# Attention on one core: where the second to fourth pairs' queries and keys are turned into fp16

## The chip, the cores and the metric

The kernel runs on one core of a Trainium2 chip. TensorE (PE) multiplies matrices and transposes, ScalarE (ACT) takes exponentials, VectorE (DVE) and GpSimd (POOL) do elementwise work, and SyncE (SP) issues transfers. The 16 DMA engines of the core move data between HBM and SBUF; transfers can be issued from SyncE, ScalarE or GpSimd, and one that changes the data type while it moves is issued from GpSimd here. The metric is the device time of one execution in microseconds.

## The reference

Attention over 8 batches of 8 heads, each with 512 queries and keys of 64 elements, in fp32:

```python
q, k, v: (8, 8, 512, 64) float32
scores = einsum('bhqd,bhkd->bhqk', q, k) / sqrt(64)
attn = exp(scores - scores.max(-1)); attn /= attn.sum(-1)
out = einsum('bhqk,bhkd->bhqd', attn, v)
```

## The kernel before

Two heads make a pair, g = 0 to 31. In each head the 512 keys are four chunks of 128. A unit is one chunk of one head: its scores, 128 keys by 512 queries, are one matmul on TensorE (`scores`, line 185). ScalarE takes the exponential of three units in one instruction (`softmax`, line 233); these groups are numbered j, and the first three are smaller. The result pt multiplies v (`weigh`, line 244, 16 products for a head), with a column of ones beside v that gives the sums; DVE divides (`normalise`, lines 257 and 258) and SyncE stores (`save`, line 266). Eight units are set aside from ScalarE and computed by polynomial on DVE with one step on GpSimd (`Aside`, lines 207 to 220); its result e is written at line 210.

For the scores, q and k must lie with the 64 elements across partitions. So the fp16 tile qk of a pair, 128 positions by 2 x 2 x 4 x 64, is transposed on TensorE (`transpose`, line 141: 16 small matmuls, those of q first, then those of k) into PSUM, and DVE copies it to tqk (line 144).

How qk and v come in:

- Pair 0: heads loaded in fp32 by SyncE and ScalarE (`load_head`), cast by several engines (`open_cast`, line 159).
- Pair 1: `load(1, "qk")` on SyncE (line 85), 256 KB each, and `cast_qk(1)` on GpSimd (line 113).
- Pairs from 2: `load_cast(g)` (line 93), two transfers issued from GpSimd that read fp32 and write fp16.
- v of every pair: `load(g, "v")` on SyncE, and `cast_v(g)` on GpSimd (line 121) into one of five buffers vps, from which the products of the pair five before must have been read.

Each engine works in the order in which the program gives it its instructions. Lines 399 to 449 write out the opening by hand. Then the loop over j (line 451) gives ScalarE its exponential, TensorE the scores of the next group, and at a pair's first unit a block: `load_cast(g + 6)`, `cast_v(g + 2)`, `load(g + 5, "v")`. `plan.fill(j)` then picks transposes, heads (products and division) and set-aside units from a table of estimated costs and times. Estimates decide the order when the program is built, and neither the transfers' queue nor their landing enters them; for the transposes a fixed time for each pair is used. In the order that comes out, the transposes of pair 2 stand on TensorE ahead of the scores of group 5, which belong to pair 1; those of pair 3 ahead of the scores of group 8; those of pair 4 behind the scores of group 9.

Of the kernel before, what the change touches and what calls it, by code (L numbers as in the profile page):

```python
# [27 lines left out]
def kernel(  # L28
# [34 lines left out]
    G = 3  # L63
    NV = 5
    AHEAD = 6

    cpool = ctx.enter_context(tc.tile_pool(name="att_const", bufs=1))
    lpool = ctx.enter_context(tc.tile_pool(name="att_load", bufs=AHEAD + 1))
    xpool = ctx.enter_context(tc.tile_pool(name="att_x", bufs=4))
# [4 lines left out]
    def rows(x, g, lo=0, hi=2):  # L74
        b, h = g // ppb, 2 * (g % ppb)
        return x[b, h + lo : h + hi].rearrange("h (p i) d -> p h (i d)", i=NI)
# [3 lines left out]
    def load(g, names="qkv"):  # L80
        if g >= n_pairs:
            return
        for nm in names:
            r = lpool.tile([P, 2, NI * D], FP32, tag=f"{nm}32", name=f"{nm}32_{g}")
            nc.sync.dma_start(out=r, in_=rows(dict(q=q, k=k, v=v)[nm], g))
            raw[g, nm] = r

    def load_cast(g):
        if g >= n_pairs:
            return  # L90
        qk = xpool.tile([P, 2, 2, NI, D], FP16, tag="qk", name=f"qk_{g}", bufs=AHEAD + 4)
        for n in range(2):
            nc.gpsimd.dma_start(  # L93
                out=qk[:, n].rearrange("p h i d -> p h (i d)"), in_=rows((q, k)[n], g)
            )
        halves[g] = qk

    def load_head(h, nm, eng):
        if ("head", h) not in raw:
            raw["head", h] = cpool.tile([P, 2 * NI, D], FP32, name=f"raw_0_{h}")  # L100
        lo = NI * "kq".index(nm)
        eng.dma_start(  # L102
            out=raw["head", h][:, lo : lo + NI].rearrange("p (o i) d -> p o (i d)", o=1),
            in_=rows(dict(q=q, k=k)[nm], 0, h, h + 1),
        )
# [4 lines left out]
    def cast_qk(g):  # L110
        qk = xpool.tile([P, 2, 2, NI, D], FP16, tag="qk", name=f"qk_{g}", bufs=AHEAD + 4)
        for n in range(2):
            nc.gpsimd.tensor_copy(
                out=qk[:, n].rearrange("p h i d -> p h (i d)"), in_=raw[g, "qk"[n]]
            )
        halves[g] = qk

    def cast_v(g):
        if g >= n_pairs:
            return  # L120
        nc.gpsimd.tensor_copy(  # L121
            out=vps[g % NV][:, :, :, 0:D],
            in_=raw[g, "v"].rearrange("p h (i d) -> p h i d", d=D),
        )

    def aux(shape, dt, name):
        return pspool.tile(shape, dt, tag="ps_x", bufs=2, name=name)
# [21 lines left out]
    def open_cast(h, eng, lo, hi):  # L149


        if ("x", h) not in raw:
            raw["x", h] = cpool.tile([P, N, D], FP16, name=f"x_0_{h}")
            f = cpool.tile([D, NI + 1, P], FP16, name=f"t_0_{h}")
            r = cpool.tile([D, FIRST, P], FP16, name=f"r_0_{h}")
            raw["t", h] = f, r
            keys = [r[:, c] for c in range(FIRST)] + [f[:, 0]]
            tqk[0, h] = (f[:, 1:].rearrange("d n p -> d (n p)"), keys)
        eng(out=raw["x", h][:, lo:hi], in_=raw["head", h][:, lo:hi])  # L159

    def open_turn(h, lo, hi, ps):
        for i in range(lo, hi):
            nc.tensor.transpose(ps[:, i - lo, :], raw["x", h][:, i, :], ident16)

    def open_copy(h, eng, lo, hi, ps):
        f, r = raw["t", h]
        t = f[:, lo - FIRST : hi - FIRST] if lo >= FIRST else r[:, lo:hi]
        eng(out=t, in_=ps[:, 0 : hi - lo])
# [7 lines left out]
    def scores(j):  # L176
        if j >= len(sizes):
            return
        if j not in st:
            st[j] = pspool.tile([P, G, S], FP32, tag="ps_st", bufs=2, name=f"st_{j}")  # L180
        for x in range(sizes[j]):
            g, c, h = units[firsts[j] + x]
            tq, tk = tqk[g, h]
            key = tk[c] if g == 0 else tk[:, c * P : (c + 1) * P]
            nc.tensor.matmul(st[j][:, x, :], key, tq, start=True, stop=True)  # L185
# [44 lines left out]
    def softmax(j):  # L230
        n = sizes[j]
        pt[j] = ppool.tile([P, G, S], FP16, tag="pt", name=f"pt_{j}")
        nc.scalar.activation(out=pt[j][:, 0:n], in_=st[j][:, 0:n], func=EXP, scale=scale)  # L233
# [46 lines left out]
    def close():  # L280
        o = pspool.tile([P, NI, W], FP32, tag="ps_st", bufs=2, name="o_last")
        weigh(last, 1, o, range(NI - 1))
        softmax(len(sizes) - 1)
        weigh(last, 1, o, [NI - 1])
        normalise(last, 1, o)
        save(last, 1, 1)
# [111 lines left out]
    with tc.manual_schedule():  # L398
        load_head(0, "q", nc.sync)
        load_head(0, "k", nc.scalar)  # L400
        load_head(1, "q", nc.sync)
        load_head(1, "k", nc.scalar)
        blank = cpool.tile([P, P], FP16, name="blank")
        nc.vector.memset(blank, 0.0)
        small = cpool.tile([P, 1], FP32, name="small")
        nc.vector.memset(small, 0.0)  # L406
        nc.scalar.activation(out=small, in_=small, func=EXP, scale=scale)
        ident16 = cpool.tile([P, P], FP16, name="ident16")
        make_identity(nc, ident16)
        load(1, "qk")  # L410
        for g in range(AHEAD - 1):
            load(g, "v")
        for n in range(NV):
            nc.vector.memset(vps[n][:, :, :, D:W], 1.0)
        def busy(tile, n):
            for _ in range(n):
                nc.tensor.matmul(tile[:, G - 1, 0:P], blank, blank, start=True, stop=True)  # L417

        busy(pspool.tile([P, G, S], FP32, tag="ps_st", bufs=2, name="warm"), 24)
        A, V, Y = nc.scalar.copy, nc.vector.tensor_copy, nc.gpsimd.tensor_copy  # L420
        open_cast(0, V, 3, 6)
        open_cast(0, A, 6, 8)
        open_cast(0, A, 0, 3)
        open_cast(1, Y, 0, 3)
        a1, a2 = (aux([D, N, P], FP16, f"open_{n}") for n in range(2))
        a3 = pspool.tile([D, N, P], FP16, tag="ps_st", bufs=2, name="open_2")
        open_turn(0, 3, 6, a1)
        open_turn(0, 6, 8, a2)
        open_turn(0, 0, 3, a3)
        open_copy(0, V, 3, 6, a1)  # L430
        open_copy(0, A, 6, 8, a2)
        open_cast(1, V, 3, 8)
        open_copy(0, V, 0, 3, a3)
        st[0] = pspool.tile([P, G, S], FP32, tag="ps_st", bufs=2, name="st_0")
        busy(st[0], 4)
        scores(0)
        scores(1)
        b1, b2 = (aux([D, N, P], FP16, f"open_{n + 3}") for n in range(2))
        open_turn(1, 3, 8, b1)
        open_turn(1, 0, 3, b2)  # L440
        open_copy(1, V, 3, 8, b1)
        open_copy(1, V, 0, 3, b2)
        load_cast(2)
        cast_qk(1)
        load_cast(3)
        cast_v(0)
        load_cast(4)
        cast_v(1)
        load_cast(5)

        for j in range(len(sizes) - 1):
            assert not plan.heads or plan.heads[0][2] > j - 7, (j, plan.heads[0])
            softmax(j)
            plan.exp(j)
            if j > 0:
                scores(j + 1)
                plan.scored(j + 1)
                if j == 2:
                    for n in range(2):
                        transpose(1, (n,))  # L460
                        plan.turned(1)
                for u in range(firsts[j - 1], firsts[j - 1] + sizes[j - 1]):
                    g, c, h = units[u]
                    if u == first_of[g]:
                        load_cast(g + AHEAD)
                        cast_v(g + 2)
                        load(g + AHEAD - 1, "v")
                    if c == (FIRST - 1 if g == 0 else NI - 1):
                        plan.heads.append((g, h, j - 1))
                plan.fill(j)  # L470
        plan.fill(len(sizes), last_call=True)
        close()
# [30 lines left out]
```

The softmax here doesn't subtract the row's maximum and nothing guards it: scores larger than these inputs give would overflow.

## Time and profile before

| what | value |
|---|---|
| median of 13 runs | 127.92 us (126.83 to 129.32) |
| the profiled execution | 127.47 us, span 125.7 us |
| ScalarE busy | 114.3 us, 91% of the span |
| TensorE busy | 110.7 us, 88% |
| VectorE busy | 85.6 us, 68% |
| GpSimd busy | 70.9 us, 56% |
| granted TensorE clock, mean | 0.966 |
| GpSimd's queue | 16320 packets, 7.87 MB |
| SyncE's queue | 18256 packets, 17.57 MB |

The span runs from the first to the last instruction; the execution's own time is 1.8 us longer. Engine times are sums of busy time and can overlap. In the rows shown below, the first number is the start in microseconds from the span's beginning, the second the duration; "out<-in" names tiles as the program does; "x8" means eight instructions in one row; square brackets give the idle time of the engine just before and what ended it. A row of transfers ends with the size of one and the median time from issue to landing.

### The profile page before, as it was taken

The page shows a single profiled execution, that of the slowest core. Times are in us where ns is not written, and L with a number is a line of the kernel's source. Part 1 is how long each engine was busy: PE and PEld are TensorE (multiplying, and loading weights), DVE is VectorE, ACT ScalarE, POOL GpSimd, SP SyncE. Part 2 cuts the span into 40 slices and gives each one's busy share as a digit, 9 for nine tenths or more (in the row PEclk, how much of TensorE's full clock was granted, in tenths as well). Part 3 has the DMA queues.
Part 4 walks back from the last instruction along what each step waited for, and adds up shares of the span by engine and source line. Part 5 has one row for each costly group of instructions (what it writes and reads, how often), then busy time and mean ns, then how long its engine had stood idle before and what let it go on. Part 6 is the DMA issues. An engine that isn't in the chain of part 4 may idle for free.

```text
span 125.7 us, 4402 instructions
## 1 busy us (share of the span) xinstructions
PE 110.7 (88%) x1820; PEld 66.8 (53%) x1820; DVE 85.6 (68%) x213; ACT 114.3 (91%) x90; POOL 70.9 (56%) x109
## 2 busy tenths in 40 slices
PE   6981999999889999998998999899998998999690
PEld 6620556555546556555555645466554554666270
DVE  0440257996986898597879769955898699465251
ACT  4593489999999999999999999999999999999980
POOL 2699990894991099179529908995099162100000
PEclk9997569999999999999999999999999999999997
DMA  4999999899999999999999998999999974224204
GB/s 124 287 331 275 205 193 203 238 144 262 204 198 170 312 247 164 250 285 145 231 250 232 208 239 264 199 261 248 276 275 156 230 199 166 89 83 167 89 13 154
DMA packets 34883, 25.97 MB, mean 207 GB/s; under 512 B 2096, under 2 KB 34864, under 8 KB 34864
## 3 DMA queue, kind: packets, MB, share of 16 engines
q0 software_dynamic: 16320, 7.87, 50.6%
q1 hardware_dynamic: 18256, 17.57, 44.1%
q8 instruction: 14, 0.23, 0.8%
q10 hardware_dynamic: 288, 0.26, 0.6%
q14 instruction: 5, 0.04, 0.1%
HBM read 25.17 MB, written 8.39 MB: 267 GB/s over the span
## 4 chain that ended last, share of the span: by engine, by line
ACT 62%; issue 16%; PE 9%; DMA 8%; DVE 1%; POOL 1%; ACTq 0%
ACT pt L233 62%; DMA qk<-in_k_dram 6%; PE o L244 4%; PE st L185 4%; DMA raw<-in_k_dram 2%; PE tps L141 1%; DVE osb L258 1%; POOL qk L93 1%; ACTq L102 0%; DVE rcp L257 0%; POOL x L159 0%; ACTq L233 0%
## 5 line engine op out<-in xcount | busy, mean ns | idle before, releaser
L233 ACT ACTIVATE pt<-st 128x1536 f16<-128x1536 f32 (+2 forms) x85 | 111.9, 1540 | 5.1 <-PE st L185 5.1
L185 PE MATMUL st<-tqk 64*128 64x512 f16 x240 | 49.4, 389 | 5.8 <-ACT pt L233 5.0
L244 PEld LDWEIGHTS <-pt 128*128 128x128 f16 x992 | 34.2, 99 | 19.3 <-issue 10.5
L244 PE MATMUL o<-vp,pt 128*128 128x65 f16 x976 | 39.4, 196 | 1.1 <-DVE osb L258 0.5
L144 DVE COPY tqk<-tps 128x1024 f16<-128x1024 f16 (+1 forms) x32 | 21.2, 670 | 11.6 <-PE tps L141 11.2
L258 DVE TENSOR_TENSOR osb<-o,rcp 128x256 f32<-128x256 f32 x63 | 26.8, 425 | 2.2
L121 POOL CAST vp<-v 128x512 f16<-128x512 f32 x32 | 21.8, 684 | 5.0 <-PE o L244 4.9
L257 DVE RECIPROCAL rcp<-o 128x4 f32<-128x4 f32 x63 | 11.3, 179 | 18.6 <-PE o L244 18.1
L141 PEld LDWEIGHTS <-qk 128*64 128x64 f16 x496 | 15.6, 112 | 15.4 <-issue 9.1
L141 PE MATMUL tps<-ident,qk 128*64 128x128 f16 x496 | 20.4, 226 | 3.7 <-DMA qk<-in_q_dram 2.0
L93 POOL DMA_DIRECT2D qk<-in_q_dram x30 | 22.1, 735 | 0.4
L210 POOL TENSOR_SCALAR e<-n 128x512 int32<-128x512 int8 x8 | 4.9, 611 | 29.9 <-DVE n L207 29.9
L93 POOL DMA_DIRECT2D qk<-in_k_dram x30 | 21.6, 719 | 0.0
L185 PEld LDWEIGHTS <-tqk 64*128 64x128 f16 x240 | 11.5, 94 | 14.1 <-issue 6.5
L220 DVE SCALAR_TENSOR_TENSOR a<-f 128x512 f32<-128x512 f32 x8 | 6.9, 856 | 0.0
L220 DVE SCALAR_TENSOR_TENSOR pa<-a,f 128x512 f16<-128x512 f32 x8 | 6.1, 768 | 0.0
L220 DVE SCALAR_TENSOR_TENSOR f<-sa,n 128x512 f32<-128x512 f32 x8 | 5.5, 691 | 0.3
L220 DVE SCALAR_TENSOR_TENSOR f<-f,e 128x512 f32<-128x512 f32 x8 | 5.5, 681 | 0.0
L207 DVE TENSOR_SCALAR n<-sa 128x512 int8<-128x512 f32 x8 | 5.4, 681 | 0.0
L417 PE MATMUL warm<-blank 128*128 128x128 f16 x24 | 2.7, 313 | 1.0 <-DVE small L406 1.0
L417 PEld LDWEIGHTS <-blank 128*128 128x128 f16 x28 | 2.7, 141 | 1.1 <-DVE small L406 1.0
L244 PEld LDWEIGHTS <-pa 128*128 128x128 f16 x32 | 1.4, 98 | 3.4 <-DVE tqk L144 1.3
(32 smaller groups left out, 21.5 us busy)
## 6 DMA issues: line engine op xcount, KB each, us to landing
v<-in_v_dram SPq DMA_DIRECT2D x32, 256.0 KB, 5.7
out_dram<-osb SPq DMA_DIRECT2D x31, 256.0 KB, 4.4
qk<-in_q_dram POOLq DMA_DIRECT2D x30, 128.0 KB, 5.6
qk<-in_k_dram POOLq DMA_DIRECT2D x30, 128.0 KB, 6.1
raw<-in_k_dram ACTq DMA_DIRECT2D x2, 128.0 KB, 2.9
raw<-in_q_dram SPq DMA_DIRECT2D x2, 128.0 KB, 2.7
q<-in_q_dram SPq DMA_DIRECT2D x1, 256.0 KB, 4.7
k<-in_k_dram SPq DMA_DIRECT2D x1, 256.0 KB, 4.9
```

Of the source, the lines that this page charges most:

```text
L93: nc.gpsimd.dma_start(out=qk[:, n].rearrange("p h i d -> p h (i d)"), in_=rows((q, k)[n], g))
L121: nc.gpsimd.tensor_copy(out=vps[g % NV][:, :, :, 0:D], in_=raw[g, "v"].rearrange("p h (i d) -> p h i d", d=D),)
L141: nc.tensor.transpose(ps[D * h : D * (h + 1), n - lo, i, :], halves[g][:, n, h, i, :], ident16)
L144: nc.vector.tensor_copy(out=turned[g][:, lo:hi], in_=ps)
L185: nc.tensor.matmul(st[j][:, x, :], key, tq, start=True, stop=True)
L207: nc.vector.tensor_scalar(out=n, in0=s, scalar1=rate, scalar2=SHIFT, op0=AluOp.mult, op1=AluOp.add)
L220: nc.vector.scalar_tensor_tensor(out=o, in0=x, scalar=k, in1=y, op0=op0, op1=op1)
L233: nc.scalar.activation(out=pt[j][:, 0:n], in_=st[j][:, 0:n], func=EXP, scale=scale)
L244: nc.tensor.matmul(o[:, i, :], p[:, i * P : (i + 1) * P], vps[g % NV][:, h, c, :], start=(c == 0 and i == blocks[0]), stop=(c == NI - 1), ...
L257: nc.vector.reciprocal(out=rcp[:, lo:hi], in_=o[:, lo:hi, D:W])
L258: nc.vector.tensor_tensor(out=o_sb[g][:, h, lo:hi], in0=o[:, lo:hi, 0:D], in1=rcp[:, lo:hi].broadcast_to([P, hi - lo, D]), op=AluOp.mult,)
L417: nc.tensor.matmul(tile[:, G - 1, 0:P], blank, blank, start=True, stop=True)
```

## The change

A constant `WIDE = 4` divides the pairs. Queries and keys of pairs 2 and 3 (the third and fourth) no longer come by `load_cast` on GpSimd's queue; as for pair 1, SyncE loads them in fp32 and GpSimd casts them with `cast_qk`. The loads of q, k and v are interleaved on SyncE: q and k of 1, v of 0, q and k of 2, v of 1, q and k of 3, v of 2, 3, 4. Casting loads start with pair 4. In the opening GpSimd now gets: casts of pair 1, v of 0, casts of pair 2, v of 1, casting loads of 4 and 5. The casts of pair 3 stand at the head of pair 0's block, and in every block the cast of v now stands before the casting load.

```diff
     AHEAD = 6
+    WIDE = 4
...
         load(1, "qk")
-        for g in range(AHEAD - 1):
+        load(0, "v")
+        for g in range(2, WIDE):
+            load(g, "qk")
+            load(g - 1, "v")
+        for g in range(WIDE - 1, AHEAD - 1):
             load(g, "v")
...
-        load_cast(2)
         cast_qk(1)
-        load_cast(3)
         cast_v(0)
-        load_cast(4)
+        cast_qk(2)
         cast_v(1)
-        load_cast(5)
+        for g in range(WIDE, AHEAD):
+            load_cast(g)
...
                     if u == first_of[g]:
+                        if g + 3 < WIDE:
+                            cast_qk(g + 3)
+                        cast_v(g + 2)
                         load_cast(g + AHEAD)
-                        cast_v(g + 2)
                         load(g + AHEAD - 1, "v")
```

## The prediction

> **What bounds the kernel now.** I read the page first, then ScalarE's and TensorE's timelines of the first 25 us, then GpSimd's, and last the DMA issues one by one. ScalarE is 91% busy (114.3 of 125.7 us). Its timeline shows where the other time is:
>
> ```profile
> 6.78 3.79 ACT L233 ACTIVATE pt<-st 128x1024 f16<-128x1024 f32 x3 [0.29 <-PE st L185]
> 14.28 2.79 ACT L233 ACTIVATE pt<-st 128x1536 f16<-128x1536 f32 x2 [3.71 <-PE st L185]
> 17.55 2.92 ACT L233 ACTIVATE pt<-st 128x1536 f16<-128x1536 f32 x2 [0.47 <-PE st L185]
> 20.64 25.63 ACT L233 ACTIVATE pt<-st 128x1536 f16<-128x1536 f32 x19 [0.17 <-PE st L185]
> ```
>
> Columns: start, duration, what, and in brackets the idle time before it and its releaser. From 20.64 on the exponentials follow each other without a gap until 118.8. So what is lost before 20.64 is lost for good, and what is saved there is saved in the end: 3.71 + 0.47 + 0.17 = 4.35 us is the most that can be had. Exponential 5 (three units of pair 1; I number them by the loop variable j) starts at 14.28 and waits for scores that TensorE writes late. TensorE's timeline says why:
>
> ```profile
> 11.09 0.50 PE L141 MATMUL tps<-ident,qk 128*64 128x128 f16 x8 [2.01 <-DMA qk<-in_q_dram]
> 12.65 0.64 PE L141 MATMUL tps<-ident,qk 128*64 128x128 f16 x8 [1.06 <-DMA qk<-in_k_dram]
> 13.21 1.46 PE L185 MATMUL st<-tqk 64*128 64x512 f16 x6
> 14.61 1.94 PE L244 MATMUL o<-vp,pt 128*128 128x65 f16 x32
> 16.48 1.03 PE L185 MATMUL st<-tqk 64*128 64x512 f16 x3
> 17.44 0.94 PE L141 MATMUL tps<-ident,qk 128*64 128x128 f16 x16
> 18.31 0.60 PE L185 MATMUL st<-tqk 64*128 64x512 f16 x3
> ```
>
> The scores of exponential 5 belong to pair 1, which is long there, but in TensorE's order they stand behind the transposes of g=2 (third pair), and those wait for q and k of g=2. The chain that ended last goes the same way, and GpSimd's timeline has the issues:
>
> ```profile
> 5.45 7.15 DMA qk<-in_k_dram
> ...
> 12.65 0.64 PE tps L141 x5
> ```
>
> ```profile
> 4.57 0.88 POOL L93 DMA_DIRECT2D qk<-in_q_dram  x1
> 5.45 0.72 POOL L93 DMA_DIRECT2D qk<-in_k_dram  x1
> 6.36 0.61 POOL L113 CAST qk<-q 128x512 f16<-128x512 f32 x1 [0.19 <-DMA q<-in_q_dram]
> 7.05 0.62 POOL L113 CAST qk<-k 128x512 f16<-128x512 f32 x1
> ...
> 9.04 0.63 POOL L121 CAST vp<-v 128x512 f16<-128x512 f32 x1
> ```
>
> The casting loads are issued late (behind a cast that waits for the head of k) and take 6.5 and 7.15 us to land, at 11.04 and 12.60. A second loss hangs on the first: the granted clock is halved in the stretch after the wait.
>
> ```profile
> 4.45:11.28 6.83, 4.59 (x48) 2.19 (x48) 2.25 (x7) 5.24 (x6) 6.55 (x11) 1.00 1.13 316
> 11.28:18.10 6.82, 5.76 (x71) 3.32 (x68) 1.91 (x5) 3.34 (x3) 6.82 (x11) 0.50 1.40 208
> 20.64:118.80 98.16, 90.90 (x1571) 54.22 (x1568) 76.78 (x181) 98.16 (x74) 55.66 (x81) 1.00 0.98 209
> ```
>
> Columns: stretch, its length, busy time of PE, PEld, DVE, ACT, POOL, the granted clock, DMA share, GB/s. With TensorE busy 4.59 of 6.83 us (67%), the next 6.83 us ran at 0.50; 32 products took 1.94 us there against 1.16 at 18.84.
>
> **The change, part by part.**
>
> 1. When q and k of g=2 arrive. They become SyncE's sixth and seventh loads, in the places that v of g=1 and g=2 have now. The second of these places was issued at 3.64 and took:
>
> ```profile
> 3.64 0.47 SPq L85 DMA_DIRECT2D v<-in_v_dram  x1
> ```
>
> ```profile
> v<-in_v_dram SPq DMA_DIRECT2D x1, 256.0 KB, 5.6
> ```
>
> So q lands at 3.13 + 5.4 = 8.5 and k at 3.64 + 5.6 = 9.2 (same shape, 256 KB). The loads of this queue land 0.7 us apart there (7.7, 8.5, 9.2). Bounds for k: 9.0, if the casting loads' traffic that begins at 8 us goes away, to 10.0, the landing of the next place.
>
> 2. The casts on GpSimd. Its order becomes: casts of g=1, v of 0, casts of g=2, v of 1, casting loads of g=4 and 5, casts of g=3, v of 2, loads of 6, v of 3, loads of 7, v of 4, loads of 8. Removed ahead of it are 4 issues of 0.72 (2.9 us), added are 4 casts of 0.62 (2.5 us). Casts of g=1 stay where they are, 6.36 to 7.67 (they wait for data). v of 0 lands at 7.75: cast until 8.45. q of g=2: 8.5 to 9.15. k: 9.25 to 9.9. Bounds of a cast: 0.61 and 1.09, the shortest and longest in the trace; I take 0.62, that of this same operation.
>
> 3. Transposes of g=2 then end at 9.9 + 0.35 = 10.25 (16 took 0.72 at full clock) instead of 13.28, three scores (0.6) follow, and exponential 5 starts at about 10.9 instead of 14.28. Exponential 4 ends at 10.57, so 0.3 of the 3.71 us stays: gain 3.4.
>
> 4. What is late next: g=3. Now its loads are issued at 7.61 and 8.33, land at 14.98, and its transposes start at 17.44, unhindered. After, q and k land on SyncE's queue at 10.6 and 11.3 (two and three steps of 0.7 behind k of g=2), but the casts stand behind v of 1 (to 10.55) and four issues (4 x 0.72, to 13.45): q until 14.1, k until 14.75. TensorE, with no stall and full clock, comes to these transposes at 13.2 (scores to 11.45, 32 products 1.16, then three scores when exponential 5 is done at 12.3). So it waits about 1.5 us for k, ends the transposes at 15.1 and the scores of exponential 8 at 15.7. Exponentials 5 to 7 (1.4 each) last until 15.1, so ScalarE waits 0.7 there. Start of exponential 8: 15.8 instead of 19.01, gain 3.2. Then, as now, 32 products and three scores (18.31 + 0.60 to 20.54, 1.63 us) lie between, and exponential 9 starts at 17.45 instead of 20.64: gain 3.2. Bounds: nothing lost at g=3 if TensorE comes later or GpSimd earlier, gain up to 4; with longest casts (6 before this point, 0.47 more each) 2.8 lost.
>
> 5. Casting loads that are later. g=4 is issued at 10.5 instead of 9.60 and needed at 17.3. Its latency was 6.0 behind a backlog, and 3.9 and 3.5 at 23.2 and 24.0 where the queue was empty; I take 4.7, landing 15.2 and 16. Loads of 6 and 7: issued at 15.4 and 17.4 instead of 13.01 and 14.99, needed at 25.48 - 3.2 = 22.3 and 26.68 - 3.2 = 23.5; with 4.8 (k 0.7 later) k lands at 20.9 and 22.9. Cost nothing, with a cover of only 1.4 and 0.6 us; if latency is the 6.5 of the opening, about 1 us of TensorE's time is lost. From g=8 on the lead is 7 us and more.
>
> 6. The scaling of the set-aside unit of g=3 (line 210) now starts at 22.54, with GpSimd idle for 3.48 us. After, GpSimd comes to it at about 20.7 (work as in 2 and 4: 15.4 + three pairs of issues at 1.43 and two casts at 0.6), when its input has been there since 19.2; the consumer on DVE stands at 25.61 - 3.2 = 22.4. Cost nothing, cover 1 us. The pattern after it recovers: GpSimd sits idle 29.9 us before these eight instructions.
>
> 7. v before the casting loads in each pair's block: the loads are issued 0.6 us later, against leads of 5 us or more. The cast could wait for products that still read its buffer; in the trace it does so twice, at 105 and 109 us, when no loads are left. Nothing. SyncE: four more issues (0.5 each, to about 9 us with the waits for landings); the first store on it is at 17.25, or 14 after. Nothing.
>
> Sum: 3.2 us. The profiled execution took 127.47 (125.7 span and 1.8 around it), which gives 124.3; it lies 0.45 below the median of the runs, 127.92, from which I get 124.7.
>
> A rule that speaks against the change: the Trainium skill, "DMA: Bandwidth & Descriptors", section "Anatomy of one DMA", has a load issued from GpSimd take about 2.0 us plus its bytes at 436 GB/s. By it k of g=2 would land about 2.6 us after its issue, at 8.1, TensorE would not wait, and the change would be worth nothing; the trace has 7.15 us, and I go by the trace.
>
> **The rivals.**
>
> A. As summed, 124.7 (124.0 to 125.4). For it: the wait is on ScalarE's path, and its end is set by a landing that moves by 3 us.
>
> B. The cast of g=3 costs nothing and the clock stays full: gain 3.9 to 4.3, 123.6 to 124.0. Against it: four issues of 0.72 in front of that cast.
>
> C. The clock is halved all the same. TensorE's gaps after: 8.46 to 9.2 (with two scores inside), 9.5 to 9.9, 13.2 to 14.75 in parts. A window of 6.83 us that has all of these is some 70% busy, the window before the drop was at 67%, and the lowest while the clock held from 18.1 to 117 was 87%, by the rows of matmuls; one that has the first two gaps alone is at 89%. Then scores, products and transposes behind 11.3 or 14.7 take 1.6 times as long, as they do now at 14.61; scores of exponential 8 end 0.8 later and those of 9 another 0.8 or so: gain 1.2 to 1.9, 126.0 to 126.7. "TensorE: Matmul & The Clock Gate" in the Trainium skill, section "Why this matters for your kernels", asks only for no gaps over some 3 us. By it C could not happen, but by it the drop at 11.28 could not either, since the longest gap before it was 2.01 us.
>
> D. Loads of g=6 or 7, or the scaling of 6, come late by a microsecond: gain 2.0 to 2.4, 125.5 to 125.9.
>
> E. The other side: GpSimd's casts are stretched beside DVE, and its lateness passes through step 6 to DVE, TensorE and ScalarE one for one. There are 11 casts before the scaling; at 1.09 instead of 0.63 they make it 5.1 us later, 1.0 is cover, and 4.1 lost against 3.2 gained is 128.8. It decides from a mean of about 1.0 us per cast. Against it: casts over 0.75 us are rare among 32 and stand beside DVE's three-operand passes, which have not begun here.
>
> F. Nothing changes: the fp32 loads arrive no sooner, since all queues share the DMA engines (share above 1 from 4.45 to 18.1). To hold, k would have to land at 12, three places behind its own. 127.9.
>
> **How the numbers follow.** A 0.60, B 0.10, C 0.12, D 0.07, E 0.07, F 0.04. The time is A's, 124.7. Low: 123.5, all of B. High: 126.6, nearly all of C; E and F (0.11) stay out. Faster by over 0.5% (A to D) 0.89, within 0.5%, about what a measurement can tell, 0.04 (F), slower 0.07 (E).
>
> **What would show it.** Right: ScalarE's wait of 3.71 falls to about 0.3, exponential 5 starts near 10.9, a new wait of 0.7 stands before exponential 8, released by transposes that waited for GpSimd's cast of g=3, exponentials run without a gap from 17.5, and the clock shows no stretch of 0.50 between 11 and 18. Wrong: k of g=2 lands after 10; casts above 0.8; a 0.50 stretch; transposes of g=4, 6 or 7 that wait for a DMA; DVE waiting for line 210.

## The result, and the profile after

The changed kernel takes 126.24 us (median of 11 runs, 124.63 to 129.35) against 128.19 for the kernel before (48 runs): a ratio of 0.9863, with a 95% interval of 0.983 to 0.9895. That is faster by 1.4%, some 1.8 us, where 3.2 us (2.5%) were forecast. The direction and the place are right; the size is a little over half. Medians here are over all executions, ratios and their intervals over the undisturbed ones of both kernels (in the fourth execution's run below, two of six).

The profiled execution took 127.85 us and lies above the kernel's median; a second one, shown further down, took 124.98. Both are needed, since a good part of the missing gain shows in the difference between them. First ScalarE's timeline in the first execution, the columns as before:

```profile
8.39 1.02 ACT L234 ACTIVATE pt<-st 128x1024 f16<-128x1024 f32 x1 [1.29 <-PE st L186]
9.67 1.45 ACT L234 ACTIVATE pt<-st 128x1536 f16<-128x1536 f32 x1 [0.26 <-PE st L186]
11.80 1.45 ACT L234 ACTIVATE pt<-st 128x1536 f16<-128x1536 f32 x1 [0.68 <-PE st L186]
13.76 10.85 ACT L234 ACTIVATE pt<-st 128x1536 f16<-128x1536 f32 x8 [0.51 <-PE st L186]
```

The wait of 3.71 us before exponential 5 is gone (0.51 is left), as forecast. But there are waits of 1.29, 0.26 and 0.68 before exponentials 2 to 4, where the kernel before had 0.29 and none. TensorE's timeline shows the reason:

```profile
6.33 1.06 PE L164 MATMUL open<-ident,x 128*64 128x128 f16 x8
7.33 1.03 PE L186 MATMUL st<-t,r 64*128 64x512 f16 x2
8.15 0.63 PE L186 MATMUL st<-t 64*128 64x512 f16 x1
8.58 1.06 PE L186 MATMUL st<-t,r 64*128 64x512 f16 x2
9.57 1.07 PE L142 MATMUL tps<-ident,qk 128*64 128x128 f16 x16
```

Eight opening transposes take 1.06 us; the same eight took 0.63 in the profile before, and two scores 1.03 instead of 0.60. TensorE ran at half clock here. Its clock record begins with full clock at 13.6 us in this execution, at 4.45 in the one before. (The clock column of the windows shows 1.00 also ahead of the first record, so there it is the duration of the matmuls that tells.) A rise to full clock after 13 us is called a late clock below, one by 6.1 us an early clock. The loads were late in this execution too: k of pair 2 landed at 10.67, where 9.2 was forecast. The cold start below parts the two.

The second execution of the same kernel, with full clock from 6.1 us:

```profile
7.37 7.81 ACT L234 ACTIVATE pt<-st 128x1024 f16<-128x1024 f32 x6 [0.44 <-PE st L186]
15.87 1.45 ACT L234 ACTIVATE pt<-st 128x1536 f16<-128x1536 f32 x1 [0.69 <-PE st L186]
17.50 8.17 ACT L234 ACTIVATE pt<-st 128x1536 f16<-128x1536 f32 x6 [0.17 <-PE st L186]
25.93 5.48 ACT L234 ACTIVATE pt<-st 128x1536 f16<-128x1536 f32 x4 [0.27 <-PE st L186]
```

Here exponentials 2 to 7 follow each other without a gap, exponential 5 starts at 11.04 (forecast 10.9), exponential 8 at 15.87 after a wait of 0.69 (15.8, 0.7), exponential 9 at 17.50 (17.45). In the kernel before exponential 9 started at 20.64: 3.14 us gained, forecast 3.2. The GpSimd rows behind it:

```profile
8.47 0.62 POOL L114 CAST qk<-q 128x512 f16<-128x512 f32 x1
9.24 0.62 POOL L114 CAST qk<-k 128x512 f16<-128x512 f32 x1
...
13.57 0.65 POOL L114 CAST qk<-q 128x512 f16<-128x512 f32 x1
14.12 0.65 POOL L114 CAST qk<-k 128x512 f16<-128x512 f32 x1
```

The casts of pair 2 run as the loads land (8.42 and 9.18), those of pair 3 end at 14.77, behind the four issues; TensorE waits for them:

```profile
14.27 0.96 PE L142 MATMUL tps<-ident,qk 128*64 128x128 f16 x16 [0.86 <-POOL qk L114]
15.17 0.60 PE L186 MATMUL st<-tqk 64*128 64x512 f16 x3
```

One wait had a price of zero in the sum: the 0.27 us before exponential 15. TensorE stands before it at the second half of pair 7's transposes, and k of pair 7, issued at 17.93, has a landing time of 6.9 us where 4.8 was taken.

```profile
24.89 0.41 PE L142 MATMUL tps<-ident,qk 128*64 128x128 f16 x8 [0.93 <-DMA qk<-in_k_dram]
```

```profile
qk<-in_k_dram POOLq DMA_DIRECT2D x1, 128.0 KB, 6.9
```

Without the wait, exponential 15 would have started 0.16 us before the end of the row ahead, as it does in the kernel before, so this takes 0.43 us of the lead (3.14 to 2.71), and from then on the two kernels run in parallel to the last exponentials: the lead at exponential 83 is still 2.73. The first execution waits 0.46 us at the same place.

### The profile page after: what moved, and what is told of

The parts are those of the page before. It is cut to its first block, busy times and chain, and to the rows that moved or that the text cites. A ratio compares the mean times of both kernels' runs of the same rounds, so it can differ in the third digit from the quotient of the medians.

```text
span 126.1 us, 4405 instructions
## 1 busy us (share of the span) xinstructions
PE 112.9 (90%) x1820; PEld 67.6 (54%) x1820; DVE 85.5 (68%) x213; ACT 114.3 (91%) x90; POOL 69.3 (55%) x109
## 4 chain that ended last, share of the span: by engine, by line
ACT 57%; issue 15%; DMA 11%; POOL 6%; PE 4%; SPq 2%; DVE 0%; ACTq 0%
ACT pt L234 57%; DMA v<-in_v_dram 6%; DMA qk<-in_k_dram 6%; POOL qk L94 4%; SPq L86 2%; PE o L245 2%; PE st L186 1%; POOL vp L122 1%; POOL qk L114 1%; PE o_last L245 1%; SPq L103 1%; DVE osb L259 0%; PE tps L142 0%; DVE rcp L258 0%; ACTq L234 0%
## 5 line engine op out<-in xcount | busy, mean ns | idle before, releaser
L122 POOL CAST vp<-v 128x512 f16<-128x512 f32 x32 | 20.7, 648 | 6.5 <-PE o L245 4.9
L94 POOL DMA_DIRECT2D qk<-in_q_dram x28 | 20.6, 735 | 0.0
L94 POOL DMA_DIRECT2D qk<-in_k_dram x28 | 20.0, 716 | 0.0
L221 DVE SCALAR_TENSOR_TENSOR f<-f,e 128x512 f32<-128x512 f32 x8 | 6.1, 765 | 0.0
L221 DVE SCALAR_TENSOR_TENSOR a<-f 128x512 f32<-128x512 f32 x8 | 5.8, 722 | 0.0
L114 POOL CAST qk<-q 128x512 f16<-128x512 f32 x3 | 1.9, 618 | 3.3 <-DMA q<-in_q_dram 3.2
```

Of the source, the lines that this page charges most:

```text
L94: nc.gpsimd.dma_start(out=qk[:, n].rearrange("p h i d -> p h (i d)"), in_=rows((q, k)[n], g))
L122: nc.gpsimd.tensor_copy(out=vps[g % NV][:, :, :, 0:D], in_=raw[g, "v"].rearrange("p h (i d) -> p h i d", d=D),)
L221: nc.vector.scalar_tensor_tensor(out=o, in0=x, scalar=k, in1=y, op0=op0, op1=op1)
```

## The experiments

In the diffs below, the kernel is the changed one unless the text says "before". Exponentials are numbered by j as in the prediction.

**The changed kernel again.** The same code, for a second profile.

> The changed kernel once more, for a second profile of it. In the first one q of pair 1, the same load at the same issue as before, landed at 7.68 us instead of 6.30, and TensorE ran at half clock up to 13.6 us. Theory A (the queue): the loads added behind it make the early loads of SyncE's queue land later; then q of pair 1 lands near 7.7 again, casts of pair 2 end near 11.3 and exponential 5 starts near 12.3. Theory B (that one execution): q of pair 1 lands near 6.3, casts of pair 2 end near 9.9, exponential 5 starts near 11, and what was missing of the 3.2 us is lost later, behind the casts of pair 3 or the casting loads of pairs 6 and 7. Either way the ratio to before is near 0.986.

Measured: ratio 0.9844 (0.9741 to 0.9948). The profile is the second one above. Theory A, that the loads put on SyncE's queue delay the ones ahead of them, falls for this execution: q of pair 1 landed at 6.28, as before the change (6.30). Over all traces this landing is between 5.8 and 7.7 in kernels with more loads on that queue, and 5.1 to 6.4 in the four with the old loads; it varies from execution to execution, and whether the queue adds a few tenths is left open.

**Casts of pair 3 ahead of the casting loads.**

```diff
         cast_qk(2)
         cast_v(1)
+        cast_qk(3)
         for g in range(WIDE, AHEAD):
             load_cast(g)
...
-                        if g + 3 < WIDE:
-                            cast_qk(g + 3)
                         cast_v(g + 2)
```

> The casts of pair 3 stand in the opening behind v of 1, ahead of the casting loads of pairs 4 and 5. Theory B with the prediction's step 4: TensorE's wait for these casts (0.7 us on ScalarE before exponential 8) goes, and the ratio to before falls from 0.986 to about 0.980, unless the casting loads, 1.2 us later, take it back. Theory A: at most 0.3 us, ratio 0.984 to 0.987, since with everything 1.4 us later TensorE hardly waits at that place.

Measured: 0.9957 (0.9907 to 1.0006), nearly all of the gain lost. ScalarE's timeline:

```profile
10.58 6.82 ACT L234 ACTIVATE pt<-st 128x1536 f16<-128x1536 f32 x5
17.78 1.45 ACT L234 ACTIVATE pt<-st 128x1536 f16<-128x1536 f32 x1 [0.38 <-PE st L186]
21.91 1.45 ACT L234 ACTIVATE pt<-st 128x1536 f16<-128x1536 f32 x1 [2.68 <-PE st L186]
23.87 1.45 ACT L234 ACTIVATE pt<-st 128x1536 f16<-128x1536 f32 x1 [0.51 <-PE st L186]
```

The wait before exponential 8 goes, as step 4 has it, and exponential 9 starts at 15.91, 1.6 us earlier than in the second execution. But the casting loads of pairs 4 and 5 are issued 1.2 us later, and TensorE is 1.6 us earlier:

```profile
19.55 1.31 PE L142 MATMUL tps<-ident,qk 128*64 128x128 f16 x16 [1.80 <-DMA qk<-in_q_dram]
20.79 1.03 PE L186 MATMUL st<-tqk 64*128 64x512 f16 x3
```

The transposes of pair 5 wait for a load issued at 13.30 that lands at 19.50, and the clock is halved from within that wait on (18.66 to 25.48). So the place of the casts of pair 3 behind four issues costs 0.7 us and saves more than that.

**Only pair 2 moved**: `WIDE = 3`.

> WIDE = 3: only pair 2 is loaded in fp32 on SyncE, pairs from 3 by casting loads. Theory A: two loads fewer on SyncE's queue, so q of pair 1 lands earlier than in the changed kernel, between 6.3 and 7.7. Theory B: it lands at 6.3 in both. Both: exponential 5 starts as in the changed kernel or earlier, but the casting loads of pair 3, issued at about 10.6, land after 15, and ScalarE waits 1 to 2 us before exponential 8: ratio 0.985 to 0.995.

Measured: 0.9867 (0.9767 to 0.9967). ScalarE's timeline:

```profile
7.82 7.05 ACT L234 ACTIVATE pt<-st 128x1536 f16<-128x1536 f32 x5
15.93 1.45 ACT L234 ACTIVATE pt<-st 128x1536 f16<-128x1536 f32 x1 [1.06 <-PE st L186]
17.55 8.45 ACT L234 ACTIVATE pt<-st 128x1536 f16<-128x1536 f32 x6 [0.17 <-PE st L186]
```

Exponential 5 starts at 10.73, exponential 8 at 15.93 after a wait of 1.06 for the casting load of pair 3, exponential 9 at 17.55. Pair 2 alone brings the gain; moving pair 3 as well changes little as far as this interval tells, since its casts come as late as its casting loads would. Exponential 15 waits 0.33 us here too.

**The order in the blocks alone**, in the kernel before:

```diff
-                        load_cast(g + AHEAD)
                         cast_v(g + 2)
+                        load_cast(g + AHEAD)
```

> The kernel before, with the cast of v ahead of the casting load in every pair's block, and nothing else of the change. All theories: no difference, ratio 0.997 to 1.003; if it is slower by 0.5% or more, the order in the blocks is what eats part of the gain.

Measured: 0.9991 (0.9936 to 1.0045). Step 7 of the prediction, which costs this at nothing, holds. The profile gave something else: full clock came only at 17.0 us there, and still exponential 9 started at 20.44, not later than the 20.64 of the execution with full clock at 4.45.

**A third execution of the changed kernel.**

> The changed kernel a third time. In its second profile exponential 9 started 3.14 us earlier than before (predicted 3.2), and 0.43 of it was lost at exponential 15, where k of pair 7 landed at 24.84. If those two numbers are of the kernel, they are seen again: exponential 9 at 17.4 to 17.6, a wait of 0.25 to 0.5 before exponential 15, a span of 123 to 123.6. If the first profile's late clock (full only from 13.6 us) comes in it again, exponential 9 starts near 19.1 and the span is 126.

Measured: 0.9832 (0.9771 to 0.9893); the profiled execution took 125.75, with a span of 124.0, longer than the expected 123 to 123.6. Exponential 9 starts at 17.36, 3.28 us before that of the kernel before; k of pair 7 landed at 23.88, and there was no wait before exponential 15, so those 0.4 us come and go. But the whole lead did not reach the end. The windows (stretch, length, busy time of PE, PEld, DVE, ACT, POOL, clock, DMA share, GB/s):

```profile
113.12:116.53 3.41, 2.40 (x20) 0.80 (x17) 0.81 (x3) 3.41 (x3) 0.00 (x0) 1.00 0.24 82
116.53:119.95 3.42, 3.42 (x58) 2.89 (x55) 1.45 (x6) 2.28 (x3) 0.00 (x0) 0.50 0.06 22
```

Near the end TensorE has less to do; after a stretch in which it was busy 2.40 of 3.41 us (70%), the next ran at half clock, with the last products in it. From exponential 9 to the end of the span it was 106.6 us here, 105.7 in the second execution and 105.1 in the profile of the kernel before, which had no such stretch. The kernel before has it too in other executions: 106.4 in the profile of the block order, with half clock from 119.4.

**Pair 4 on SyncE too**: `WIDE = 5`.

> WIDE = 5: pair 4 too is loaded in fp32 on SyncE and cast on GpSimd. Two issues of 0.72 fewer stand ahead of the casts of pair 3, and pair 4 no longer hangs on a casting load. Theory of the order on GpSimd (step 4): casts of pair 3 end near 13.3 instead of 14.77, the wait of 0.7 before exponential 8 goes, exponential 9 starts near 16.7, and the ratio falls by 0.005 to 0.007 against the changed kernel. Rival: the stall only moves on, as with the casts of pair 3 put first, to pair 5, whose casting load is the first in the queue now and is issued at 10.6: then a wait of more than 0.5 before exponential 10 to 12.

Measured: 0.9735 (0.9657 to 0.9814). The wait before exponential 8 is gone, exponential 9 starts at 16.31, and 0.46 us are waited before exponential 11, for pair 5: the theory of the order on GpSimd holds, and most of the rival's wait is there as well. The ratio is 0.010 below that of the third execution's run, where 0.005 to 0.007 were expected; the two intervals overlap.

**Pairs 2 to 5 on SyncE**: `WIDE = 6`.

> WIDE = 6: pairs 2 to 5 on SyncE, casting loads from pair 6 on. Step 5's theory (casting loads of 6 and 7 land too late since they are issued late): loads of 7 are issued near 15.8 instead of 17.2, and the wait before exponential 15 goes (0.4 us). Against it the casts of pair 5 stand at 17.2 to 18.5 on GpSimd, where TensorE wants them at about 17.8: a wait of about 0.7 before exponential 11. Ratio 0.978 to 0.986.

Measured: 0.9739 (0.965 to 0.9827), below the expected 0.978 to 0.986. The wait before exponential 15 is gone, as step 5's theory has it, and the one before exponential 11 is 0.06. In this execution q of pair 1 landed late (7.40) and the clock was halved from 10.9 to 14.3, so exponential 5 started at 12.71, with waits of 1.08 and 1.07 before exponentials 4 and 5; the profile can't show what the kernel does when the loads land early.

**The kernel before with the wait filled.**

```diff
         for n in parts:
+            for x in range((50, 25)[n] if g == 2 else 0):
+                nc.tensor.transpose(ps[:, n - lo, x % NI, :], blank, ident16)
             for i in range(NI):
```

> The kernel before, with 50 and 25 transposes of a blank tile ahead of the transposes of q and of k of pair 2, where TensorE waits for the casting loads. It parts the late landing from the halved clock that followed it. If the clock falls because TensorE stood idle: no stretch of 0.50 between 11 and 18, exponential 5 still starts near 14 (the landing), and exponential 9 0.6 to 0.9 us earlier than 20.64: ratio 0.993 to 0.995. If the fall has another cause, nothing changes.

Measured: 1.002 (0.998 to 1.006). TensorE's and ScalarE's timelines:

```profile
9.62 2.97 PE L140 MATMUL tps<-ident,blank 128*128 128x128 f16 x50
12.52 0.41 PE L143 MATMUL tps<-ident,qk 128*64 128x128 f16 x8
12.86 1.57 PE L140 MATMUL tps<-ident,blank 128*128 128x128 f16 x25
14.36 0.41 PE L143 MATMUL tps<-ident,qk 128*64 128x128 f16 x8
```

```profile
15.35 6.82 ACT L235 ACTIVATE pt<-st 128x1536 f16<-128x1536 f32 x5 [4.17 <-PE st L187]
```

There were too many: the blank transposes end 1.3 us after q has landed (11.24) and 1.6 after k (12.74), so exponential 5 is late by 1.07. But the clock stayed full from 6.1 us to the end of the work, and from exponential 5 to 9 it is 5.33 us instead of 6.36. With TensorE kept busy the clock did not fall there; its fall after the wait had cost 1.0 us, more than the 0.64 of waits counted in the prediction, since without a wait each exponential starts 0.1 us before the row ahead of it ends. The gain and the delay cancel (exponential 9 at 20.68 and 20.64), so the ratio tells nothing by itself. The changed kernel, too, is above 5.33 between exponentials 5 and 9 (6.45 us in its second execution): about as much as it saves on the clock there goes to the wait for the casts of pair 3.

**A cold start**, in the changed kernel and in the one before: one blank matmul instead of 24 in front.

```diff
-        busy(pspool.tile([P, G, S], FP32, tag="ps_st", bufs=2, name="warm"), 24)
+        busy(pspool.tile([P, G, S], FP32, tag="ps_st", bufs=2, name="warm"), 1)
```

> The changed kernel with one blank matmul instead of 24 in front, so that TensorE's clock rises late in every execution. Theory C2 (the prediction took the full clock in the opening from one profile; where the clock rises late, the changed kernel pays for it, since its opening now waits for TensorE and no longer for a landing): exponential 9 between 18 and 19.2 instead of 17.4, the time 1 to 2 us above the changed kernel's, ratio to before 0.99 to 1.00. Rival (the clock in the opening costs nothing, as SyncE's landings and GpSimd's casts set the pace): 0.983 to 0.987 as the changed kernel.

> The kernel before with one blank matmul instead of 24. Theory C2: its opening waits for the casting loads whatever TensorE's clock is; exponential 9 stays between 20.3 and 20.8 and the ratio at 0.997 to 1.004. If the late clock costs as much here as in the changed kernel (1 us and more, ratio over 1.008), it can't be what ate part of the gain.

Measured: 0.9843 (0.9817 to 0.9869) for the changed kernel, 0.9973 (0.9908 to 1.0037) for the one before. Full clock came at 13.3 and 17.1 us. ScalarE's timeline of the changed kernel:

```profile
9.51 1.45 ACT L234 ACTIVATE pt<-st 128x1536 f16<-128x1536 f32 x1 [0.26 <-PE st L186]
11.64 1.45 ACT L234 ACTIVATE pt<-st 128x1536 f16<-128x1536 f32 x1 [0.68 <-PE st L186]
13.51 9.51 ACT L234 ACTIVATE pt<-st 128x1536 f16<-128x1536 f32 x7 [0.42 <-PE st L186]
```

and of the kernel before:

```profile
11.67 1.45 ACT L233 ACTIVATE pt<-st 128x1536 f16<-128x1536 f32 x1 [0.68 <-PE st L185]
14.42 2.79 ACT L233 ACTIVATE pt<-st 128x1536 f16<-128x1536 f32 x2 [1.30 <-PE st L185]
17.48 6.92 ACT L233 ACTIVATE pt<-st 128x1536 f16<-128x1536 f32 x5 [0.27 <-PE st L185]
```

Exponential 9 starts at 18.84 in the changed kernel, 1.3 to 1.5 us later than with an early clock, though its loads landed early (q of pair 1 at 5.77, k of pair 2 at 8.83); the late landings of the first execution are not needed for the loss. In the kernel before it starts at 20.27, not later than with an early clock (20.64): much of the half clock lies beside the wait for the casting loads, and the early clock is lost again behind that wait. When k of pair 2 has landed (12.60 with the early clock, 12.74 here), TensorE runs at half clock until 18.1 in the one case and until 17.1 in the other. So by the traces theory C2 holds, on two executions of each kernel with a late clock (18.84 and 19.10; 20.27 and 20.44): the late clock costs the changed kernel some 1.4 us and the one before nothing, and the lead at exponential 9 is 1.4 instead of 3.2.

The time was missed: 1 to 2 us above the changed kernel's were expected, and its median, 126.16, is the changed kernel's own. Its four times lie between 125.99 and 126.39, where many of the changed kernel's lie. That many of these had a late clock too would explain it, and the mean granted clocks on record fit. The mean counts the time ahead of the first clock record as full clock: it is 0.993 for the traced cold start, half clock until 13.3 us and all. A recorded stretch of 3.41 us at 0.50 brings it to 0.986 or lower (3.41 x 0.5 of some 124 us). Of the 27 executions of the changed kernel on record 15 have 0.992 or more. Four of these took 124.41 to 124.98 us, as the second execution did, and eleven 125.45 to 126.32, up to the times of the cold start (granted clock 0.993 to 0.996). So no recorded fall held up the eleven. A late clock would do it; so might late loads, and none of the eleven was traced, so this part is argued, not shown.

**A fourth execution, beside WIDE = 5 with more rounds.**

> The changed kernel a fourth time, beside WIDE = 5, with more rounds. Ratio 0.982 to 0.987. Its trace adds one more execution: exponential 9 at 17.4 to 17.6 if the clock is full before 6.2 us, later if the clock rises later (theory C2), and the wait before exponential 15 between 0 and 0.5 with the landing of k of pair 7.

> The kernel with WIDE = 5 once more, with more rounds, beside the changed kernel on the same chip. It had 0.9735 with four runs. If that holds, 0.970 to 0.978, and 0.005 to 0.010 below the changed kernel; exponential 9 near 16.3, a wait of about 0.5 before exponential 11 for the casting load of pair 5.

Measured: 0.9768 (0.9708 to 0.9829) for the changed kernel, 0.9737 (0.9696 to 0.9777) for WIDE = 5, whose interval covers the earlier 0.9735. The first lies below the 0.982 to 0.987 expected, and the two are only 0.003 apart (0.005 to 0.010 expected); but the median of the changed kernel's six times, 127.21, is far above the 125.01 of WIDE = 5. The profiled execution of the changed kernel took 127.86, and shows one reason:

```profile
8.90:12.32 3.42, 2.78 (x51) 1.65 (x52) 0.90 (x3) 3.01 (x3) 3.12 (x5) 1.00 1.10 350
12.32:15.73 3.41, 1.80 (x32) 1.00 (x29) 1.01 (x5) 3.14 (x3) 3.41 (x7) 1.00 1.29 263
15.73:19.14 3.41, 3.41 (x38) 1.92 (x35) 1.89 (x5) 1.45 (x1) 3.41 (x7) 0.50 1.16 184
```

```profile
16.64 1.45 ACT L234 ACTIVATE pt<-st 128x1536 f16<-128x1536 f32 x1 [1.18 <-PE st L186]
19.42 2.79 ACT L234 ACTIVATE pt<-st 128x1536 f16<-128x1536 f32 x2 [1.33 <-PE st L186]
```

The clock was full from 5.5 us, but TensorE, waiting for the casts of pair 3, was busy only 1.80 of 3.41 us (53%), and the next stretch ran at half clock. Exponential 9 starts at 19.42, not at 17.4 to 17.6, although the clock was early. This is the prediction's rival C.

The second trace of WIDE = 5:

```profile
7.95 11.15 ACT L234 ACTIVATE pt<-st 128x1536 f16<-128x1536 f32 x8
19.89 5.48 ACT L234 ACTIVATE pt<-st 128x1536 f16<-128x1536 f32 x4 [0.79 <-PE st L186]
25.67 2.79 ACT L234 ACTIVATE pt<-st 128x1536 f16<-128x1536 f32 x2 [0.31 <-PE st L186]
```

Exponentials 3 to 10 run without a gap worth a row, exponential 9 starts at 16.03, and pair 5's casting load costs 0.79. This version beats both kernels in the medians of both its runs (125.11 and 125.01).

The traced executions of the two kernels, with those of the block order and the cold starts (us; "half clock" as far as the records and the durations of matmuls show it, a fall after the last product left out; the waits before exponential 15, 0.46 us in the first execution and 0.27 in the second, are in the fourth column):

| execution | half clock | exponential 9 | from there to the end | time |
|---|---|---|---|---|
| before, the profile shown | to 4.5; 11.3 to 18.1 | 20.64 | 105.1 | 127.47 |
| before, block order | to 17.0; 119.4 to 122.8 | 20.44 | 106.4 | 128.60 |
| before, cold start | to 17.1; 119.5 to 122.9 | 20.27 | 106.3 | 128.47 |
| changed, first | to 13.6; from 119.4 | 19.10 | 107.0 | 127.85 |
| changed, second | to 6.1 | 17.50 | 105.7 | 124.98 |
| changed, third | to 3.9; 116.5 to 119.9 | 17.36 | 106.6 | 125.75 |
| changed, fourth | to 5.5; 15.7 to 19.1; 118.1 to 121.5 | 19.42 | 106.7 | 127.86 |
| changed, cold start | to 13.3 | 18.84 | 105.4 | 125.99 |

## Why the prediction was right, and where its size was off

- **The bound and the lever** (the casting loads of pair 2, which TensorE waits for ahead of pair 1's scores): right. With the load elsewhere the wait of 3.71 goes in every trace (at most 0.51 is left in the five of the changed kernel), and pair 2 alone brings it. The 4.35 us called the most that can be had were too few: with the casts of pair 3 first, exponential 9 starts at 15.91, 4.73 us earlier than before, since the halved clock had cost more than the waits that were counted.
- **Steps 1 to 4** (landing of k at 9.2, casts until 9.9, exponential 5 at 10.9, casts of pair 3 until 14.75, exponential 8 at 15.8, exponential 9 at 17.45): 9.18, 9.86, 11.04, 14.77, 15.87 and 17.50 in the execution with no half clock after 6.1 us. The 3.2 us are 3.14 and 3.28 there and in the third.
- **The term that was mis-sized** is step 4's "with no stall and full clock". The opening was costed with TensorE's full clock, as in the one profile at hand. The kernel before hides a late clock behind its wait; the change takes that cover away, and nothing was costed for the cover that was gone. With a late clock the lead at exponential 9 is 1.4 to 1.5 us (20.27 to 18.84 between the two cold starts, 20.64 to 19.10 between the two first profiles). How many executions had one is not known, so how much of the missing 1.4 us of the median this term holds is not shown.
- **Rival C** (clock halved all the same, 0.12): its mechanism is seen in one of four executions of the changed kernel. There TensorE was busy 2.78 + 1.80 of 6.83 us, 67% as ahead of the fall in the profile before; some 70% had been worked out for it. That share does not decide it, though: in the third execution TensorE was busy 2.63 + 2.02 of 6.82 us (68%, 7.31 to 14.13), and the clock held. In the fourth execution exponential 9 was 1.9 to 2.1 us later than in the second and third; 1.3 to 2.0 were priced. The measured median, 126.24, lies in this rival's range (126.0 to 126.7) and not in A's (124.0 to 125.4), at the upper end of the stated range; that it meets C's figure is in part luck, since 15 of the 27 executions have a granted clock that leaves no room for such a fall.
- **Step 5** (casting loads of 6 and 7): latency taken as 4.8, measured 4.2 for pair 6 and 6.9 for k of pair 7 in the second execution; the cover of 0.6 us was too thin: a wait of 0.27 us there, which takes 0.43 of the lead, one of 0.46 in the first, none in the third and fourth. For pair 4, 4.7 was taken and 5.7 and 5.3 measured, without a wait. Rival D, at 0.4 instead of about 1 us.
- **Steps 6 and 7**: nothing, as costed. GpSimd came to the set-aside unit's step at 20.73 (20.7), and the block order alone makes 0.9991.
- **Rivals B, E, F**: the wait before exponential 8 was 0.69, 0.78 and 1.18 in the three executions with an early clock (B not seen); GpSimd's casts of q, k and v in the opening took 0.61 to 0.65 (E not seen); k of pair 2 landed at 9.18, 9.11 and 9.62 in the later executions, and at 10.67 in the first, past the bound of 10.0 but not at 12 (F not seen).
- **The end** was not in the sum: half clock near the end costs either kernel 1 to 1.5 us in some executions (the last exponential starts 1.7 to 2.4 us after the one before it instead of 1.33, and the last products take longer). The profile of the kernel before, on which the sum stood, had none.

What stays open: how often each of these comes, and what the rarest of the changed kernel's executions were (129.35 to 129.50, three of 27; none was traced). Their mean granted clocks, 0.957 to 0.966, would be some 9 to 11 us of recorded half clock, an estimate from these means and their spans of 127.6 and 127.7 us.

## What to carry to other kernels

Before a wait is costed as removable, look at what lies beside it: a slow clock, a late cast or a late load that it hid becomes the next bound, and one profile may not show it. Where transfers are moved to another queue and the cast to an engine, the order on that engine is the change: the casts of pair 3 put 3 us earlier on GpSimd undid most of the gain, because the casting loads behind them came later while TensorE came sooner. The long stage that ScalarE bounds here kept a lead to the tenth of a microsecond (2.71 us at exponential 15, 2.73 at 83), so in such a stage compare the start times of its instructions by number: that tells opening, stage and end apart when total times scatter.

## What was not expected of the hardware

- TensorE was busy by its rows, nearly without a break, from 1.0 to 13.6 us in the first profile of the changed kernel (1.00 in each of the last two stretches of 3.41 us), and the clock rose only at 13.6; in the block-order run, with one stretch of 73% on the way, at 17.0. In other executions of the same code it rose at 3.9 to 6.1.
- The clock fell with no idle time over 2.0 us: in stretches of 3.41 us, after 34% busy in the profile before (7.87 to 11.28), 53% in the fourth execution, 57% with `WIDE = 6` (7.46 to 10.88), 59% with the casts of pair 3 first (15.24 to 18.66), and 70% near the end of seven traces. It held after 56% with `WIDE = 3` (11.21 to 14.62), 59% in the third execution (10.72 to 14.13), and near the end after 70% with `WIDE = 6` (113.27 to 116.69) and 72% in the profile before (117.1 to 120.5). So the busy share of the rows by itself does not tell here when the clock falls. "TensorE: Matmul & The Clock Gate" in the Trainium skill, section "Why this matters for your kernels", asks for no gaps over some 3 us; these falls came with shorter ones.
- A load of 256 KB issued at 1.64 us as the third on SyncE's queue landed between 5.1 and 7.7 us in 14 traces.
- A casting load of 128 KB took 3.5 us from issue to landing in the profile before (issued at 24.0) and 8.6 in the run with the casts of pair 3 first (issued at 17.96), with 256 KB loads and stores under way beside it.
